# One-hot rows of the expert gates: from three engines to two, with their keys in PSUM

## The chip, the cores and the metric

The kernel runs on one core of a Trainium2 chip. Five engines work beside each other, each through its own queue in order: TensorE (PE, matrix products), VectorE (DVE), ScalarE (ACT), GpSimd (POOL) and SyncE (SP, which only issues transfers). The metric is the device time of one execution in microseconds, median of several runs.

## The reference, cut to what matters

One decoder block on 1024 tokens of width 1024 (with 16 meta tokens ahead): a convolution branch and an RWKV-7 branch, mixed by gates, and then a product-key expert layer (PEER). Only the last concerns the change. Each token has 8 heads; each head picks 16 of 16384 experts by two keys of 128, so a token has 128 pairs of an expert `e = i1 * 128 + i2` and a gate.

```python
e = (i1 * PEER_NKEYS + i2).reshape(TOK_BLOCK, PEER_HEADS * K)
gate = jax.nn.softmax(best_s, axis=-1).reshape(TOK_BLOCK, PEER_HEADS * K)
u = expert_u[e]
act = jax.nn.gelu(jnp.einsum('td,ted->te', xb, u), approximate=False)
coef = (gate * act.astype(jnp.float32)).astype(xb.dtype)
return jnp.einsum('te,ted->td', coef, expert_v[e])
```

## The kernel before, in words

The 1024 tokens are 8 tiles of 128, in two halves: tiles 0 to 3 and 4 to 7. The front part of the block and the routing (`mix_and_route`, with `top16` and `route`) run for the first half, then for the second. The expert layer is then done in two ways.

Tiles 0 to 2 are gathered (`gather_rows`): for each of a token's 128 experts an indirect transfer issued by GpSimd (L1002) brings the expert's two rows; VectorE multiplies one with the token and sums (L1005, the row product), ScalarE makes the gelu and the gate (L1006, L1007), VectorE adds the other row times the result (L997, the row sum). Tile 0's gather has the lowest priority, so it fills what the routing and the spread leave; it must be done before the dense part, which puts tile 3's result in tile 0's buffer (`hr3` under the tag `hr0`).

Tiles 4 to 7 and tile 3 are done densely: products with all 16384 experts in 128 blocks of 128, and gates that are zero but for 128 of them. For tiles 4 to 7 `u_stage` computes gelu(x u) of a block; 56 of the 128 blocks (`PRE`) are computed ahead and stored (`gs`). Tile 3's activations are computed by gathering (`gather_coefs`) and lie, times its gates, in `coef`.

`spread_gates` (L1042 on) makes the dense gates, and is what the change edits. For each tile it transposes the expert's two keys and the gates (`src[0]`, `src[1]`, `src[2]`), and for each token multiplies two one-hot matrices on TensorE: `o2` has a one where the second key is, `o1` the gate where the first key is. Work goes in quartets of four tokens, 32 quartets a tile, 160 in all. One VectorE instruction (L1076) compares `src[1]` of four tokens with `iota`, the numbers 0 to 127 in SBUF. The four `o1` rows are compared and scaled one by one (L1085): of tiles 4 to 7 (`hf` is 1) VectorE makes two, GpSimd the third, and ScalarE the fourth in two steps, an absolute difference (L1082) and a Relu (L1083); of tile 3 VectorE makes three and GpSimd one. Four products (L1087) go to one PSUM bank, `pg`, which ScalarE evicts (L1088) to `gt`, the 32 tokens of a group side by side. A group's first blocks are copied to `direct` tiles (L1090), the rest is written to DRAM (`gd`, L1091). The tiles come in the order 4, 5, 6, 7, 3 (`DT`).

The dense part (`dense`) takes four blocks at a time, multiplies the activations with the gates (L1134), splits the product into two parts for TensorE (`split`: ScalarE L224, then GpSimd L225) and adds the products with the experts' rows (L1161). Its tiles take over the memory in which the spread's lay.

Products at full precision take three passes (`mm3`, L228 to L230) over operands that ScalarE and GpSimd have split; `ul` and `vlo` are such low parts, made by GpSimd.

The order of each engine's queue is fixed when the program is built: a planner simulates the program, takes for each engine the ready instruction that stands first in program order (shifted by `high_priority` offsets), and adds waits where tiles depend on each other. So `PRE` blocks, the spread and tile 0's gather are interleaved by the planner's own times.

Of the kernel before, what the change touches and what calls it, by code (L numbers as in the profile page):

```python
# [10 lines left out]
F32 = mybir.dt.float32  # L11
# [3 lines left out]
AF = mybir.ActivationFunctionType  # L15
OP = mybir.AluOpType
# [4 lines left out]
P = 128  # L21
# [15 lines left out]
DT = list(range(4, 8)) + list(range(NGT, 4))  # L37
# [95 lines left out]
def body(tc, a, out):  # L133
    nc = tc.nc
    V, A, G, PE, SY = nc.vector, nc.scalar, nc.gpsimd, nc.tensor, nc.sync

    def pool(es, name, bufs=1, space=None, side=None):
        kw = {}
        if space is not None:
            kw["space"] = space  # L140
        if side is not None:
            kw["side"] = side
        return es.enter_context(tc.tile_pool(name=name, bufs=bufs, reuse_waits="tile", **kw))
# [40 lines left out]
    iota = cst[:, C_IOTA:C_IOTA + P]  # L184
# [858 lines left out]
    def spread_gates(es, direct):  # L1043

        gtp = pool(es, "gtp", 2)
        sb = pool(es, "sg_", 2)
        ps_ = pool(es, "sgp", 2, PSUM)
        for s_, tt in enumerate(DT):
            hf, tl = divmod(tt, 4)
            src = []  # L1050
            for k in range(3):
                f = sb.tile([P, P], F32, name="gsrc", tag="gsrc")
                if k < 2:
                    ii = sb.tile([P, P], I32, name="gint", tag="gint")
                    V.tensor_single_scalar(ii, idx[hf][:, tl], 7 if k == 0 else 127,
                                           op=OP.logical_shift_right if k == 0 else OP.bitwise_and)
                    V.tensor_copy(f, ii)
                else:
                    f = gate[1][:, tl] if hf else coef[0]
                pt = ps_.tile([P, P], F32, name="gtp")  # L1060
                PE.transpose(pt, f, ident)
                ft = sb.tile([P, P], F32, name=f"gT{k}")
                A.activation(ft, pt, AF.Copy)  # L1063
                src.append(ft)
            neg = []
            for k in (0, 2):
                nt = sb.tile([P, P], F32, name=f"ng{k}")
                V.tensor_scalar_mul(nt, src[k], -1.0)
                neg.append(nt)
            for g in range(P // GT):  # L1070
                gt = gtp.tile([P, P, GT], F32, name="gt")
                for q in range(GT // 4):
                    pg = ps_.tile([P, 4, P], F32, name="pg", bufs=3)
                    t0 = GT * g + 4 * q
                    o2 = sb.tile([P, 4, P], F32, name="o2h", bufs=3)
                    V.tensor_tensor(o2, src[1][:, t0:t0 + 4, None].to_broadcast([P, 4, P]),  # L1076
                                    iota[:, None, :].to_broadcast([P, 4, P]), op=OP.is_equal)
                    o1 = sb.tile([P, 4, P], F32, name="o1h", bufs=3)
                    for x in range(4):
                        t = t0 + x  # L1080
                        if x == 3 and hf:
                            A.activation(o1[:, x], iota, AF.Abs, bias=neg[0][:, t:t + 1])  # L1082
                            A.activation(o1[:, x], o1[:, x], AF.Relu, scale=neg[1][:, t:t + 1], bias=src[2][:, t:t + 1])  # L1083
                        else:
                            (G if x >= 2 + (not hf) else V).tensor_scalar(o1[:, x], iota, src[0][:, t:t + 1], src[2][:, t:t + 1],  # L1085
                                                               op0=OP.is_equal, op1=OP.mult)
                        PE.matmul(pg[:, x], o2[:, x], o1[:, x], start=True, stop=True)  # L1087
                    A.activation(gt[:, :, 4 * q:4 * q + 4].rearrange("p i t -> p t i"), pg, AF.Copy)  # L1088
                for k, d in enumerate(direct):
                    A.activation(d[:, P // GT * s_ + g], gt[:, GB * k:GB * k + GB], AF.Copy)  # L1090
                A.dma_start(gd[P // GT * s_ + g][:, GB * len(direct):], gt[:, GB * len(direct):])  # L1091
# [137 lines left out]
    with ExitStack() as e0:  # L1229
        spread_gates(e0, direct)  # L1230
# [21 lines left out]
```

## Time and profile before

| | us |
|---|---|
| median of three runs | 3814.73 (3814.04 to 3827.25) |
| the profiled execution, its own time | 3849.75 |
| its span, first to last instruction | 3848.0 |

The profile is of one execution. A group's row gives line, engine, operation, tiles (written <- read), shape, count, then busy time in us with the mean ns of one, then the engine's idle time before them with what ended it. A row of a line's own view gives shortest, median and longest in ns. A row of the timeline gives start and length in us, and in brackets idle time before it. A row of stretches gives length and the busy time and count of TensorE's products, its weight loads, VectorE, ScalarE and GpSimd, then the granted TensorE clock, the share of the transfer engines and GB/s.

### The profile page before, as it was taken

Reading aid. Unit: us, or ns where it says so; the run is one execution under the profiler, and the core shown is the slowest. Engines: PE = TensorE matmul, PEld = TensorE weight load, DVE = VectorE, ACT = ScalarE, POOL = GpSimd, SP = SyncE. Lnnn points to the kernel's source line nnn. Section 1 sums busy time; section 2 is a strip of 40 time slices with the busy share of each in tenths; the row PEclk is TensorE's granted clock in tenths of the full one; section 3 lists DMA queues with packets and bytes.
Section 4 is the critical chain, followed back from the end, with each engine's and each line's share of the span. In section 5 each row is a group of like instructions: output and inputs, shape, how many; then the busy total and the mean of one; then the engine's idle time right before and its main releaser. Section 6 shows DMA issues by size and latency. Waiting matters only on the chain. (4 is left out here: it accounts for less than half of the span.)

```text
span 3848.0 us, 49366 instructions
## 1 busy us (share of the span) xinstructions
PE 3378.2 (88%) x16175; PEld 2692.2 (70%) x16175; DVE 2784.9 (72%) x5150; ACT 1602.1 (42%) x3647; POOL 2405.1 (63%) x2123
## 2 busy tenths in 40 slices
PE   7999998798889987788788885899989999889997
PEld 7887775686667765676677764777777777667776
DVE  3655549789986668899999997666666666656763
ACT  5455432334443332432377764333333343333343
POOL 3442315446786548556799996666766666666773
PEclk9999978999897878989899997999999999999998
DMA  4321114424676668744677777888888878888993
GB/s 150 108 62 52 53 50 141 138 79 157 211 228 213 189 232 307 268 151 170 224 284 270 286 274 276 302 292 306 317 301 311 310 279 299 298 307 309 333 311 107
DMA packets 343126, 861.38 MB, mean 224 GB/s; under 512 B 53304, under 2 KB 132800, under 8 KB 290900
## 3 DMA queue, kind: packets, MB, share of 16 engines
q0 software_dynamic: 75328, 475.06, 34.6%
q1 hardware_dynamic: 252420, 322.48, 26.4%
q10 hardware_dynamic: 15120, 60.68, 4.0%
q8 instruction: 128, 2.10, 0.2%
q14 instruction: 130, 1.06, 0.1%
HBM read 774.33 MB, written 83.77 MB: 223 GB/s over the span
## 5 line engine op out<-in xcount | busy, mean ns | idle before, releaser
L1002 POOL DMA_INDIRECT row<-euv,idx x384 | 422.4, 1100 | 345.7 <-DVE yr L997 168.9
L225 POOL TENSOR_TENSOR vlo<-vraw,vhi 128x512 fp32r<-128x512 f32 x256 | 327.9, 1295 | 235.7 <-ACT vhi L224 215.6
L1005 DVE SCALAR_TENSOR_TENSOR row<-row,xr 128x1024 f32<-128x1024 f32 x256 | 311.5, 1218 | 179.0 <-DMA row<-euv,idx 168.9
L997 DVE SCALAR_TENSOR_TENSOR yr<-row,act,yr 128x1024 f32<-128x1024 f32 x256 | 329.6, 1288 | 153.1 <-ACT act L1007 146.4
L1006 ACT ACTIVATE act<-act 128x1 f32<-128x1 f32 x384 | 77.0, 200 | 813.8 <-DVE row L1005 813.4
L225 POOL TENSOR_TENSOR ul<-ur,uh 128x512 fp32r<-128x512 f32 x256 | 337.4, 1325 | 41.3 <-ACT uh L224 39.4
L228 PE MATMUL py<-vhi,c 128*128 128x512 f32 x640 | 265.7, 420 | 87.0 <-DVE hbuf L1161 45.2
L230 PE MATMUL zp<-x,ul 128*128 128x512 f32 x736 | 299.4, 407 | 20.6 <-POOL ul L225 20.6
L228 PE MATMUL zp<-x,uh 128*128 128x512 f32 x736 | 298.9, 406 | 4.9 <-ACT g L1099 4.8
L229 PE MATMUL zp<-x,uh 128*128 128x512 f32 x736 | 297.7, 404 | 0.0
L228 PE MATMUL zp<-vhi,c 128*128 128x512 f32 x640 | 254.0, 406 | 29.6 <-DVE hbuf L1161 22.5
L230 PE MATMUL py<-vhi,c 128*128 128x512 f32 x640 | 259.9, 412 | 21.8 <-POOL c L225 21.8
L224 ACT ACTIVATE vhi<-vraw 128x512 fp32r<-128x512 f32 x256 | 159.0, 626 | 270.7 <-DMA vraw<-euv 126.6
L229 PE MATMUL py<-vlo,c 128*128 128x512 f32 x640 | 262.9, 411 | 4.5 <-POOL vlo L225 4.5
L1087 PE MATMUL pg<-o1h,o2h 128*128 128x128 f32 x1280 | 198.8, 295 | 70.3 <-DVE o1h L1085 39.9
L229 PE MATMUL zp<-vlo,c 128*128 128x512 f32 x640 | 254.3, 401 | 0.1
L1085 POOL TENSOR_SCALAR o1h<-cst,gT,gT 128x128 f32<-128x128 f32 x160 | 249.5, 1563 | 7.1 <-ACT gT L1063 3.1
L230 PE MATMUL zp<-vhi,c 128*128 128x512 f32 x640 | 251.9, 402 | 0.0
L1087 PEld LDWEIGHTS pg<-o1h,o2h 128*128 128x128 f32 x1280 | 179.0, 202 | 100.3 <-POOL o1h L1085 37.7
L349 DVE SCALAR_TENSOR_TENSOR cy<-u,vec,cy 128x512 f32<-128x512 f32 x240 | 242.2, 1009 | 5.4
L997 DVE SCALAR_TENSOR_TENSOR hr<-row,act,hr 128x1024 f32<-128x1024 f32 x128 | 212.5, 1660 | 30.1 <-ACT act L1007 29.6
L1024 POOL DMA_INDIRECT row<-euv,twice x128 | 157.5, 1231 | 118.5 <-DVE row L1026 77.0
(1646 smaller groups left out, 9732.4 us busy)
## 6 DMA issues: line engine op xcount, KB each, us to landing
ur<-eut SPq DMA_DIRECT2D x256, 256.0 KB, 5.9
vraw<-euv SPq DMA_DIRECT2D x256, 256.0 KB, 5.7
gd<-gt ACTq DMA_DIRECT2D x20, 1920.0 KB, 7.9
gblk<-gd SPq DMA_DIRECT2D x30, 1024.0 KB, 16.2
wbr<-w_in SPq DMA_DIRECT2D x64, 256.0 KB, 3.3
wqr<-w_q SPq DMA_DIRECT2D x64, 256.0 KB, 2.9
wrr<-w_in SPq DMA_DIRECT2D x56, 256.0 KB, 2.7
gs<-g SPq DMA_DIRECT2D x56, 256.0 KB, 4.3
```

The costliest lines, as they stand in the source:

```text
L224: A.activation(hi, src, AF.Copy)
L225: return eng.tensor_sub(lo, src, hi.bitcast(F32))
L228: PE.matmul(ps, whi, xhi, start=first, stop=False)
L229: PE.matmul(ps, whi, xlo, start=False, stop=False)
L230: PE.matmul(ps, wlo, xhi, start=False, stop=last)
L349: V.scalar_tensor_tensor(y, u[:, j:j + 512], cw, y, op0=OP.mult, op1=OP.add)
L997: V.scalar_tensor_tensor(y, row[:, 1], act[:, j:j + 1], y, op0=OP.mult, op1=OP.add)
L1002: G.indirect_dma_start(out=row.rearrange("p a d -> p (a d)"), out_offset=None, in_=a["euv"], in_offset=bass.IndirectOffsetOnAxis(ap=idx[0] ...
L1005: V.scalar_tensor_tensor(row[:, 0], row[:, 0], 1.0, xn, op0=OP.mult, op1=OP.mult, accum_out=aj)
L1024: G.indirect_dma_start(out=row, out_offset=None, in_=a["euv"].rearrange("e (k d) -> (e k) d", k=2), in_offset=bass.IndirectOffsetOnAxis(ap ...
L1085: (G if x >= 2 + (not hf) else V).tensor_scalar(o1[:, x], iota, src[0][:, t:t + 1], src[2][:, t:t + 1], op0=OP.is_equal, op1=OP.mult)
L1087: PE.matmul(pg[:, x], o2[:, x], o1[:, x], start=True, stop=True)
```

## The change

A PSUM tile `keys` gets a copy of `iota`; all comparisons of the spread read it. GpSimd's rows are made by VectorE: three of four in tiles 4 to 7, all four in tile 3. The tiles come in the order 3, 4, 5, 6, 7 (each keeps its slot `s_` in the gates). The eviction's two patterns are exchanged: it reads `pg` with a stride and writes runs of four neighbouring words, where it read in order and wrote single words 32 apart.

```diff
         ps_ = pool(es, "sgp", 2, PSUM)
-        for s_, tt in enumerate(DT):
+        keys = ps_.tile([P, P], F32, name="keys", bufs=1)
+        A.activation(keys, iota, AF.Copy)
+        for s_, tt in sorted(enumerate(DT), key=lambda x: x[1]):
...
                     V.tensor_tensor(o2, src[1][:, t0:t0 + 4, None].to_broadcast([P, 4, P]),
-                                    iota[:, None, :].to_broadcast([P, 4, P]), op=OP.is_equal)
+                                    keys[:, None, :].to_broadcast([P, 4, P]), op=OP.is_equal)
...
                         if x == 3 and hf:
-                            A.activation(o1[:, x], iota, AF.Abs, bias=neg[0][:, t:t + 1])
+                            A.activation(o1[:, x], keys, AF.Abs, bias=neg[0][:, t:t + 1])
                             A.activation(o1[:, x], o1[:, x], AF.Relu, scale=neg[1][:, t:t + 1], bias=src[2][:, t:t + 1])
                         else:
-                            (G if x >= 2 + (not hf) else V).tensor_scalar(o1[:, x], iota, src[0][:, t:t + 1], src[2][:, t:t + 1],
-                                                               op0=OP.is_equal, op1=OP.mult)
+                            V.tensor_scalar(o1[:, x], keys, src[0][:, t:t + 1], src[2][:, t:t + 1], op0=OP.is_equal, op1=OP.mult)
                         PE.matmul(pg[:, x], o2[:, x], o1[:, x], start=True, stop=True)
-                    A.activation(gt[:, :, 4 * q:4 * q + 4].rearrange("p i t -> p t i"), pg, AF.Copy)
+                    A.activation(gt[:, :, 4 * q:4 * q + 4], pg.rearrange("p t i -> p i t"), AF.Copy)
```

## Rows read from the trace of the kernel before

**Rows 1.** The page's part 1: busy us, share of the span, instructions.
```profile
span 3848.0 us, 49366 instructions
...
PE 3378.2 (88%) x16175; PEld 2692.2 (70%) x16175; DVE 2784.9 (72%) x5150; ACT 1602.1 (42%) x3647; POOL 2405.1 (63%) x2123
```
**Rows 2.** Busy time by stretch: second routing, spread, seam, dense part.
```profile
1650.00:1901.00 251.00, 204.84 (x816) 161.41 (x815) 249.46 (x859) 77.46 (x159) 154.88 (x99) 0.89 0.51 173
1901.00:2342.00 441.00, 369.23 (x2088) 313.61 (x2087) 427.44 (x698) 317.28 (x675) 412.07 (x281) 0.95 0.75 273
2342.00:2390.00 48.00, 22.14 (x76) 16.79 (x77) 30.41 (x33) 16.79 (x41) 25.52 (x23) 0.67 0.91 331
2390.00:3790.00 1400.00, 1284.29 (x5341) 1026.74 (x5340) 901.19 (x1197) 487.68 (x1232) 945.82 (x885) 0.96 0.86 301
```
**Rows 3.** Groups by shape in the spread's stretch, 1901 to 2342 us.
```profile
L1085 POOL TENSOR_SCALAR o1h<-cst,gT,gT 128x128 f32<-128x128 f32 x160 | 249.5, 1563 | 7.1 <-ACT gT L1063 3.1 <-issue 1.2 <-PE pg L1087 1.2
...
L1088 ACT ACTIVATE gt<-pg 128x512 f32<-128x512 f32 x160 | 173.4, 1090 | 40.6 <-PE pg L1087 40.2
L1085 DVE TENSOR_SCALAR o1h<-cst,gT,gT 128x128 f32<-128x128 f32 x352 | 163.0, 514 | 0.0
L1076 DVE TENSOR_TENSOR o2h<-gT,cst 128x512 f32<-128x512 f32 x160 | 147.5, 923 | 4.4 <-PE pg L1087 4.4
...
L1082 ACT ACTIVATE o1h<-cst,ng 128x128 f32<-128x128 f32 x128 | 47.1, 369 | 1.0 <-DVE ng L1068 1.0
```
**Rows 4.** Line L1087: what TensorE sat idle for before it (us, times).
```profile
  POOL o1h L1085: 65.5, 80
  DVE o1h L1085: 48.3, 50
```
**Rows 5.** Lines' own views, 1901 to 2342 us: shortest, median, longest ns.
```profile
L1085 DVE TENSOR_SCALAR o1h<-cst,gT,gT x352: 331/364/2211, 1910.6 to 2338.2; 128x128 f32<-128x128 f32 x176
...
L1076 DVE TENSOR_TENSOR o2h<-gT,cst x160: 673/680/3793, 1901.7 to 2337.0; 128x512 f32<-128x512 f32 x160
...
L997 DVE SCALAR_TENSOR_TENSOR hr<-row,act,hr x53: 1269/1274/3078, 1899.9 to 2338.4; 128x1024 f32<-128x1024 f32 x53
...
L1005 DVE SCALAR_TENSOR_TENSOR row<-row,xng x54: 1207/1212/4334, 1906.0 to 2341.9; 128x1024 f32<-128x1024 f32 x54
```
**Rows 6.** Timeline, 1993 to 1997 us: two on VectorE, one on GpSimd.
```profile
1993.36 0.59 DVE L1085 TENSOR_SCALAR o1h<-cst,gT,gT 128x128 f32<-128x128 f32 x2
...
1994.48 2.47 DVE L1085 TENSOR_SCALAR o1h<-cst,gT,gT 128x128 f32<-128x128 f32 x2
...
1995.49 1.30 POOL L225 TENSOR_TENSOR ul<-ur,uh 128x512 fp32r<-128x512 f32 x1
```
**Rows 7.** VectorE groups of the whole span, then two lines' own views.
```profile
L1134 DVE TENSOR_TENSOR g<-g,gblk 128x512 f32<-128x512 f32 x56 | 49.1, 877 | 83.8 <-DMA g<-gs 83.5
...
L1134 DVE TENSOR_TENSOR g<-py,gblk 128x512 f32<-128x512 f32 x36 | 24.8, 688 | 12.2 <-ACT py L1099 9.1 <-POOL c L225 2.5 <-issue 0.4
...
L474 DVE TENSOR_SCALAR m<-pp x12: 159/676/692, 79.3 to 1205.5; 128x512 f32<-128x512 f32 x8, 128x16 f32<-128x16 f32 x4
...
L347 DVE TENSOR_SCALAR cy<-u,vec x8: 531/932/1655, 151.1 to 680.7; 128x512 f32<-128x512 f32 x8
```
**Rows 8.** Groups by shape in the second routing, 1650 to 1901 us.
```profile
L997 DVE SCALAR_TENSOR_TENSOR hr<-row,act,hr 128x1024 f32<-128x1024 f32 x21 | 44.6, 2124 | 1.3 <-ACT act L1007 1.3
...
L1005 DVE SCALAR_TENSOR_TENSOR row<-row,xng 128x1024 f32<-128x1024 f32 x20 | 31.5, 1573 | 0.0
```
**Rows 9.** Timeline at 2350 us: VectorE's last part of a product, then ScalarE.
```profile
2350.33 0.08 DVE L1005 DVE_READ_ACCUMULATOR row<-row,xng 128x1 f32 x1
...
2350.45 0.20 ACT L1006 ACTIVATE act<-act 128x1 f32<-128x1 f32 x1 [6.78 <-DVE row L1005]
```
**Rows 10.** A ScalarE eviction with contiguous ends, group of the whole span.
```profile
L961 ACT ACTIVATE qT<-acc 128x512 f32<-128x512 f32 x32 | 18.6, 581 | 0.0
```
**Rows 11.** The chain of waits, 2330 to 2400 us: start, length, what.
```profile
2341.61 11.30 DMA gd<-gt
```

## The prediction

> **What bounds the kernel now.** The page first: of a span of 3848 us VectorE is busy 72% and TensorE 88%, so no engine bounds the whole [rows 1]. A table of busy time by stretch says where the change falls. The spread of the gates lies between 1901 and 2342 us; there VectorE is busy 427 of 441 us, GpSimd 412, TensorE 369, ScalarE 317. VectorE was already full before it, in the second half's routing (249.5 of 251 us from 1650), and has room again only when the dense part runs (901 of 1400), where TensorE is the full engine (1284 of 1400) [rows 2]. So from 1650 to 2342 time is VectorE's sum of instructions, whatever their order, and a microsecond off that sum moves the start of the dense part, and with it the end, by one.
>
> Next, that stretch's groups by shape: what is VectorE's sum made of? 352 one-hot rows `o1h` and 160 one-hot tiles `o2h`, besides 54 row products and 53 row sums of tile 0's gather; GpSimd makes 160 `o1h` at 1563 ns each [rows 3, 5]. The waits of the spread's matmuls name both makers: 65.5 us until a GpSimd `o1h`, 48.3 us until a VectorE one [rows 4]. Those 65.5 us are no gain by themselves: TensorE has 72 us of slack in the stretch.
>
> What makes VectorE's sum larger than its work: the mean of each group stands far above its median. `o1h` 514 against 364 ns, `o2h` 923 against 680 [rows 3, 5]. In order of time the cause is seen: two `o1h` take 0.59 us at 1993.36, the next two 2.47 us, and they end when the `ul` split on GpSimd, begun at 1995.49, ends [rows 6]. The excess in this stretch is (514 - 364) x 352 = 52.8 us and (923 - 680) x 160 = 38.9 us: 92 us of 441.
>
> **The change, part by part.**
>
> *Keys in PSUM: the stalls go.* That a VectorE instruction with one input in PSUM escapes them is shown by the gates' multiply: with both inputs in SBUF it takes 877 ns, with one in PSUM 688, in the same stage beside the same GpSimd work [rows 7]. Bounds of the gain: 0 (the stalls follow the output, not the input) to 92 us; I take all 92, as the row is of the same kind.
>
> *Keys in PSUM: each read is slower.* 512 elements in SBUF with two per-partition scalars take 531 ns at best, 128 take 331 [rows 5, 7]: 0.52 ns an element. From PSUM 512 elements take 676 ns, 16 take 159 [rows 7]: 1.04 ns. So an `o1h` gains 128 x 0.52 = 67 ns, from 336 to 403. `o2h` is a two-input operation at 1.04 ns an element already: no change. 352 x 0.067 = 23.6 us. Bounds: 0 and 46 us (twice).
>
> [...]
>
> *160 rows come over from GpSimd.* In a run VectorE starts the second of two `o1h` 0.26 us after the first (0.59 less 0.33) [rows 6]; with 0.067 it is 0.32 us. 160 x 0.32 = 51.2 us. Together: -92 + 24 + 51 = **-17 us**. GpSimd loses 249.5 us of work [rows 3]; what it keeps, gather issues and splits, was nowhere the bound, so this is worth nothing in itself.
>
> *Fourth tile first.* Its gates don't come from the second half's routing, so its spread may start while routing still fills VectorE. It frees nothing there, but takes the place of gather rows, whose priority is lowest. Those cost most there: a row sum 2124 ns and a product 1573, against medians of 1274 and 1212 later [rows 5, 8]: 21 x 0.85 + 20 x 0.36 = 25 us. Bounds 0 (buffers held by the routing keep the tile waiting) and 25; I take half, **-12 us**. Nothing of the dense part gets later by it: after the last eviction `gd`'s write still stands in the way for 11.3 us, because the dense part's tiles lie where `gt` lay [rows 11]. TensorE is idle there; the first two products of gates and `g`, which now wait for the last tile, take 0.69 us each [rows 7] and fit in.
>
> *ScalarE's `Abs` reads the same bank.* If its reads of `keys` are put in order with VectorE's, the change adds a wait: `Abs` of a quartet after VectorE's third `o1h`, and VectorE's next `o2h` after that `Abs`. Queued behind the waiting `o2h` is all of VectorE, rows included unless the planner put one in between. A handover costs 0.04 us each way (a product ends at 2350.41, ScalarE starts 2350.45) [rows 9]. With a gather row in the gap I charge only two handovers: 128 x 0.08 = **+10 us**. Rows suffice: 53 sums and 54 products [rows 5] for 128 gaps.
>
> *Evictions.* 160 at 1.09 us write words 32 apart; the nearest with contiguous ends takes 0.58 [rows 3, 10]. Now PSUM is read with a stride instead: no row shows it. Bounds 0.58 and 1.60 us (both penalties); I take 0.65, nearer the contiguous row. ScalarE, at 317 of 441 us, hides either; without cover the upper end is 82 us on ScalarE.
>
> Sum: -17 - 12 + 10 = **-19 us**, all on VectorE's path. Against the profiled execution's own 3849.8 us that is 3830; the median of the runs is 35 us below it, so 3814.7 - 19 = 3796 us.
>
> **Rivals.**
>
> *The two readers alternate (slower).* In each of 128 quartets VectorE waits for `Abs`: 0.37 us [rows 3], two handovers, and the overlap of 0.08 us that a dependent instruction loses: 0.53 us; ScalarE, 72% busy, adds some 0.2. Unfilled that is 128 x 0.73 = 93 us against 29 saved: +64. It decides from about 40 unfilled gaps (40 x 0.73 = 29). For it: ScalarE's queue is in order too, so a late `Abs` also holds evictions back; the planner knows neither the stalls nor, perhaps, the eviction's real time, so its rows may fall beside the gaps. Against: as many rows as gaps. With two thirds unfilled, +33: 3848 us. [...]
>
> *No difference.* What is won is lost again: the tile starts no earlier, -17 + 10 = -7; or a read from PSUM costs twice the 67 ns, 512 x 0.067 = 34 us more on the forecast, +15. That is 3808 to 3830 us. The PSUM row speaks against the second [rows 7]. [...]
>
> *Larger gain.* All 25 us of dear rows leave the routing, the readers are not ordered, and the last gather rows slip under the write of `gd`: -17 - 25 - 13 = -55, 3760 us. TensorE's slack (72 us) allows it. Against: it takes all three.
>
> **How the numbers follow.** Forecast (3775 to 3812): 0.45; alternating readers: 0.30; no difference: 0.12; larger gain: 0.13. What a measurement can tell from no change is 0.5%, 19 us, so the forecast itself lies on that line. Faster: 0.25 of the forecast, 0.13, and 0.02 of the third, 0.40. Same: 0.20, 0.04 of the alternation (gaps half filled), 0.08: 0.32. Slower: 0.26 and 0.02: 0.28. Range for 8 in 10: 3755 (all gains) to 3860 (three quarters of the gaps open); the forecast's own range is 3775 to 3812.
>
> **What would show it.** `o1h` on VectorE x512 at a mean near 400 ns and hardly above its median, `o2h` at 680; no GpSimd instruction at the one-hot line; row products and sums with a mean still above the median. The first `o2h` before 1895 us if the tile's head start works. Waits of VectorE's `o2h` for ScalarE's `Abs`, by their count and total, decide between forecast and alternation: under 30 us for the forecast. Evictions near 0.65 us. The last matmul of the spread near 2320 instead of 2340 us. Wrong, if the spread's stretch is longer than 441 us, if `o1h` from PSUM has a median over 470 ns, or if VectorE is idle in it for more than 50 us.

## The result, and the profile after

The changed kernel takes 3851.9 us (median of 11 runs, 3827.6 to 3871.3); the kernel before, timed beside it, 3821.3 (11 runs, 3806.2 to 3835.3). The ratio is 1.0074, 95% interval 1.0046 to 1.0103: **slower by 28 us** (the medians differ by 31), where 19 us less were forecast. The time is near that of the first rival, in which the two readers alternate (3848 us).

The page of the profile after, part 1, to compare with [rows 1]:
```profile
span 3858.2 us, 49060 instructions
...
PE 3409.8 (88%) x16175; PEld 2717.4 (70%) x16175; DVE 2759.2 (72%) x5310; ACT 1567.0 (41%) x3648; POOL 2150.0 (56%) x1963
```
GpSimd lost 255 us and ScalarE 35 us of work, VectorE 26 us. Nobody works more except TensorE, whose 16175 products took 32 us more at a lower granted clock (0.914 over the span, 0.922 before; see the last section), and yet the execution is longer. So the loss is first looked for as idle time in the stage that was changed.

The profiled spans differ by 10 us only, because the profile of before fell above all of its timed runs, and what lies ahead of the stored blocks differs by up to 39 us between the traces (their first product starts at 1681 to 1720 us). So kernels are compared here over a stretch that every trace has: from the first product of the stored blocks (`zp` from the second half) to the last product of the spread, and from there to the first product of the dense part (`py`). Busy time of the two stretches before (columns as in [rows 2]):
```profile
1720.00:2340.50 620.50, 516.19 (x2664) 427.98 (x2662) 606.44 (x1223) 371.24 (x786) 530.26 (x355) 0.94 0.69 247
2340.50:2362.10 21.60, 0.02 (x2) 0.02 (x1) 13.02 (x15) 6.05 (x20) 9.65 (x9) 0.50 0.95 361
```
The same two after, and as third row the end of the first:
```profile
1717.00:2369.90 652.90, 555.29 (x2664) 456.23 (x2662) 605.84 (x1400) 341.96 (x806) 287.68 (x203) 0.88 0.68 250
2369.90:2382.10 12.20, 0.04 (x1) 0.00 (x0) 8.58 (x11) 8.30 (x20) 4.27 (x5) 0.54 0.60 224
2283.00:2370.00 87.00, 69.91 (x320) 55.75 (x320) 64.60 (x158) 58.88 (x130) 0.64 (x2) 0.83 0.35 143
```
The first stretch grew by 32.4 us. VectorE's busy time in it is the same (606.4 and 605.8), its idle time rose from 14.1 to 47.1 us: the stretch is longer because VectorE waits. The same sum of work hides an exchange: the one-hots take 25 us less, and 74 row sums and 73 products lie in the stretch, 19 us more than the 68 of each before; the rest of the work in it is 5 us more. The seam (from the spread's last product to the dense part's first) gave 9.4 us back: five products and five sums of tile 0 lay in it before, and now tile 0 is done long ahead of it. The third row shows where most of the waiting is: for the last 87 us GpSimd has next to nothing to do (0.6 us), the transfers are at 143 GB/s, and VectorE is idle for 22 us.

What VectorE waited for, its groups after, 1650 to 2420 us:
```profile
L1087 DVE TENSOR_SCALAR o1h<-keys,gT,gT 128x128 f32<-128x128 f32 x512 | 176.7, 399 | 0.0
L1005 DVE SCALAR_TENSOR_TENSOR row<-row,xng 128x1024 f32<-128x1024 f32 x78 | 122.0, 1564 | 13.4 <-DMA row<-euv,idx 13.2
L997 DVE SCALAR_TENSOR_TENSOR hr<-row,act,hr 128x1024 f32<-128x1024 f32 x79 | 119.6, 1514 | 1.6 <-ACT act L1007 1.6
L1078 DVE TENSOR_TENSOR o2h<-gT,keys 128x512 f32<-128x512 f32 x160 | 108.8, 680 | 28.4 <-ACT o1h L1084 28.0 <-issue 0.4
```
L1084 is ScalarE's `Abs`: 28.0 us. The one-hot instructions have no stall left: `o1h` 399 ns (514 in [rows 3]) and `o2h` 680 (923).

The line of `o2h` by itself in the last 87 us, its durations and what ended VectorE's idle time before it (us, times):
```profile
L1078 DVE TENSOR_TENSOR o2h<-gT,keys x39: 686/687/689, 2283.8 to 2366.8; 128x512 f32<-128x512 f32 x39
...
  ACT o1h L1084: 20.9, 39
```
All 39 quartets wait, 0.54 us each. Of the 121 before them, 32 (tile 3's) have no `Abs`, and the other 89 wait 16 times. The difference is the gather rows: on VectorE nothing else is left to fill a gap. The line of the row products shows when they ran out:
```profile
L1005 DVE SCALAR_TENSOR_TENSOR row<-row,xng x78: 1196/1218/3462, 1650.6 to 2270.5; 128x1024 f32<-128x1024 f32 x78
```
Tile 0's last product starts at 2270.5 us, 99 us before the spread ends. Before, one still ended at 2350.41 [rows 9], after the spread. In order of time the tail looks like this (timeline at 2320 us; in brackets idle time and what ended it):
```profile
2319.63 0.72 DVE L1087 TENSOR_SCALAR o1h<-keys,gT,gT 128x128 f32<-128x128 f32 x2
...
2320.39 0.37 ACT L1084 ACTIVATE o1h<-keys,ng 128x128 f32<-128x128 f32 x1
2320.78 0.69 DVE L1078 TENSOR_TENSOR o2h<-gT,keys 128x512 f32<-128x512 f32 x1 [0.43 <-ACT o1h L1084]
...
2321.39 1.04 DVE L1087 TENSOR_SCALAR o1h<-keys,gT,gT 128x128 f32<-128x128 f32 x3
2322.16 0.60 ACT L1089 ACTIVATE gt<-pg 128x512 f32<-128x512 f32 x1 [0.89 <-PE pg L1088]
2322.66 0.36 ACT L1084 ACTIVATE o1h<-keys,ng 128x128 f32<-128x128 f32 x1
2323.05 0.69 DVE L1078 TENSOR_TENSOR o2h<-gT,keys 128x512 f32<-128x512 f32 x1 [0.62 <-ACT o1h L1084]
```
VectorE's third `o1h` ends at 2322.43. `Abs` could follow, but an eviction stands ahead of it in ScalarE's queue, so that it starts at 2322.66. It ends at 2323.02, and `o2h`, which waited 0.62 us for it, starts at 2323.05.

ScalarE's groups after, 1880 to 2380 us, give the other direction and the evictions:
```profile
L1089 ACT ACTIVATE gt<-pg 128x512 f32<-128x512 f32 x160 | 94.0, 591 | 58.3 <-PE pg L1088 56.0 <-DVE idx L841 1.7
...
L1084 ACT ACTIVATE o1h<-keys,ng 128x128 f32<-128x128 f32 x128 | 46.9, 367 | 59.6 <-DVE o1h L1087 58.8
```
`Abs` waits 58.8 us for VectorE's `o1h`, for which it waited not at all before [rows 3]; an eviction takes 591 ns instead of 1090 [rows 3].

### The profile page after: what moved, and what is told of

Same layout as the page of the kernel before. It is cut to its first block, busy times and chain, and to the rows that moved or that the text cites. A ratio compares the mean times of both kernels' runs of the same rounds, so it can differ in the third digit from the quotient of the medians.

```text
span 3858.2 us, 49060 instructions
## 1 busy us (share of the span) xinstructions
PE 3409.8 (88%) x16175; PEld 2717.4 (70%) x16175; DVE 2759.2 (72%) x5310; ACT 1567.0 (41%) x3648; POOL 2150.0 (56%) x1963
## 3 DMA queue, kind: packets, MB, share of 16 engines
q14 instruction: 127, 1.04, 0.1%
## 4 chain that ended last, share of the span: by engine, by line
PE 25%; DVE 20%; DMA 15%; issue 13%; POOL 8%; ACT 2%; SPq 1%; POOLq 0%; DVEq 0%; ACTq 0%
DMA row<-euv,idx 7%; DMA vraw<-euv 4%; PE zp L228 4%; PE zp L229 3%; PE zp L230 3%; DVE row L1005 2%; PE py L228 2%; DMA g<-gs 2%; DVE hr L997 2%; PE py L229 2%; PE py L230 2%; POOL vlo L225 2%; PE pg L1088 1%; POOL row L1002 1%; POOL row L1024 1%
## 5 line engine op out<-in xcount | busy, mean ns | idle before, releaser
L1002 POOL DMA_INDIRECT row<-euv,idx x384 | 412.2, 1073 | 530.4 <-DVE yr L997 238.8
L1088 PE MATMUL pg<-o1h,o2h 128*128 128x128 f32 x1280 | 251.1, 334 | 73.9 <-DVE o1h L1087 46.4
L230 PE MATMUL zp<-x,ul 128*128 128x512 f32 x736 | 297.7, 404 | 11.4 <-POOL ul L225 11.3
L1088 PEld LDWEIGHTS pg<-o1h,o2h 128*128 128x128 f32 x1280 | 219.3, 227 | 119.7 <-issue 40.6
L1005 DVE SCALAR_TENSOR_TENSOR row<-row,xng 128x1024 f32<-128x1024 f32 x128 | 204.0, 1594 | 34.0 <-DMA row<-euv,idx 33.8
L1026 DVE SCALAR_TENSOR_TENSOR row<-row,xng 128x1024 f32<-128x1024 f32 x128 | 185.2, 1454 | 57.1 <-DMA row<-euv,twice 56.7
```

Of the source, the lines that this page charges most:

```text
L230: PE.matmul(ps, wlo, xhi, start=False, stop=last)
L1002: G.indirect_dma_start(out=row.rearrange("p a d -> p (a d)"), out_offset=None, in_=a["euv"], in_offset=bass.IndirectOffsetOnAxis(ap=idx[0] ...
L1005: V.scalar_tensor_tensor(row[:, 0], row[:, 0], 1.0, xn, op0=OP.mult, op1=OP.mult, accum_out=aj)
L1026: V.scalar_tensor_tensor(row, row, 1.0, xn, op0=OP.mult, op1=OP.mult, accum_out=act[:, j:j + 1])
```

## The experiments

Each was timed beside the kernel before, whose median was 3821.6, 3822.2 and 3824.7 us in the three groups of runs; ratios are to that kernel, and differences in us are between medians where nothing else is said. "Theory 1" is that the order of the two readers is the loss; its rivals are the order in which the filling work runs out, and VectorE's sum.

**1. `Abs` from SBUF, all else as changed.**
```diff
-                            A.activation(o1[:, x], keys, AF.Abs, bias=neg[0][:, t:t + 1])
+                            A.activation(o1[:, x], iota, AF.Abs, bias=neg[0][:, t:t + 1])
```


> The changed kernel, but ScalarE's Abs reads the numbers in SBUF, so VectorE is the only reader of the PSUM keys. Theory 1 (the two readers alternate, and this is the loss): the 28.0 us in which VectorE's o2h waited for Abs and the 58.8 us in which Abs waited for VectorE's o1h vanish; the spread ends some 28 us earlier, near 2342 us, and the time is near 3824 us, level with the kernel before. Theory 2 (the loss is the order of the fillers: the stored blocks and tile 0's gather run out early and leave the last 97 us of the spread alone): the waits vanish too, but the tail is still alone and is bound by another latency; at most 10 us come back, 3842 us or more. Theory 3 (VectorE's sum of instructions grew by the rows from GpSimd): no change, 3852 us.

3807.0 us, ratio 0.9965 (0.9944 to 0.9985): 45 us off the changed kernel (42 by the ratios), more than the 28 us of visible waits and than the 28 us expected. The stretch to the last product of the spread is
```profile
1714.30:2319.80 605.50, 521.60 (x2664) 441.32 (x2662) 598.75 (x1398) 322.08 (x800) 279.21 (x200) 0.91 0.74 263
```
and VectorE's groups of the row products and of `o2h`, 1650 to 2420 us, are
```profile
L1005 DVE SCALAR_TENSOR_TENSOR row<-row,xng 128x1024 f32<-128x1024 f32 x77 | 120.6, 1567 | 4.7 <-DMA row<-euv,idx 4.7
...
L1078 DVE TENSOR_TENSOR o2h<-gT,keys 128x512 f32<-128x512 f32 x160 | 108.2, 676 | 0.0
```
VectorE is idle for 6.8 us instead of 47.1. Of these 40 us, 28 were waits for `Abs` and some 9 waits of row products for their transfers (13.4 against 4.7). The two profiled executions themselves lie 36 us apart. The second theory (the fillers' order by itself) and the third (VectorE's sum) fall: with the readers apart the gather lasts to the end of the spread again (its last product starts at 2315.5 us), so its running out was a consequence of the filled gaps.

**2. The readers in two banks.** The transposes at a tile's start give up one of their two banks.
```diff
+        keya = ps_.tile([P, P], F32, name="keya", bufs=1)
+        A.activation(keya, iota, AF.Copy)
...
-                pt = ps_.tile([P, P], F32, name="gtp")
+                pt = ps_.tile([P, P], F32, name="gtp", bufs=1)
...
-                            A.activation(o1[:, x], keys, AF.Abs, bias=neg[0][:, t:t + 1])
+                            A.activation(o1[:, x], keya, AF.Abs, bias=neg[0][:, t:t + 1])
```


> The changed kernel, but ScalarE's Abs reads a second copy of the keys in a PSUM bank of its own; the bank comes from the transposes at a tile's start, which get one instead of two. Theory (what costs is that two engines' reads of one bank are put in order): no waits between o2h and Abs, 3807 us as with Abs from SBUF, within 8 us. Rival (an Abs from PSUM is itself what delays VectorE or ScalarE): 3852 us.

3808.2 us, 0.9961 (0.9939 to 0.9984): the same as from SBUF. So ScalarE's read of PSUM costs nothing here (`Abs` takes 362 ns on average, 393 from SBUF in experiment 1, and `o2h` does not wait for it); the shared tile in one bank does (28.0 us of waits). The copy and its bank came together here, so which of the two sharings makes the order is not shown.

**3. The old order of the tiles**, in the changed kernel and, second, with `Abs` from SBUF.
```diff
-        for s_, tt in sorted(enumerate(DT), key=lambda x: x[1]):
+        for s_, tt in enumerate(DT):
```


> The changed kernel with the tiles in the old order 4, 5, 6, 7, 3. As predicted, the head start is worth 12 us, so its loss costs that: 3864 us. Rival: the head start only exchanges gather rows against quartets and is worth nothing; and since tile 3 has no ScalarE row, it comes last as a tail without alternation, where 39 waits of 0.54 us (20.9 us) stood: 3852 - 21 = 3831 us.

> The changed kernel with Abs from SBUF and the tiles in the old order, so that the order is seen without the two readers. Theory (the head start is worth nothing, as it was beside the alternation): the time of the order-new twin, 3807 us, within 8 us. Rival as predicted: the head start is worth 12 us, 3819 us. Third: the old order is the better one without the alternation, since tile 3 has the longest sum on VectorE and the spread of the others then hides it: 3795 us.

3848.9 us, 1.0079 (1.0048 to 1.0109), and 3807.6 us, 0.9964 (0.9936 to 0.9993): each as its twin in the new order (3851.9 and 3807.0). The head start is worth nothing that can be told: the intervals of the two pairs together leave an estimated 10 us either way. A tail without alternation (tile 3 last) doesn't help either: in the first of the two VectorE's waits for `Abs`, in the four other tiles, are still 19.1 us, and those of row products for their transfers 17.7; the last row product starts at 2229.8 us, and the spread's last product at 2344.

**4. The new evictions alone**, in the kernel before.
```diff
-                    A.activation(gt[:, :, 4 * q:4 * q + 4].rearrange("p i t -> p t i"), pg, AF.Copy)
+                    A.activation(gt[:, :, 4 * q:4 * q + 4], pg.rearrange("p t i -> p i t"), AF.Copy)
```


> The kernel before with the new eviction patterns alone. Evictions take 0.60 us instead of 1.09, ScalarE loses 160 x 0.49 = 78 us of work. Theory as predicted: ScalarE is not the bound in the spread, so no change, within 5 us of the kernel before. Rival: the 40.2 us in which evictions waited for products and the held pg buffers passed on to TensorE and VectorE, so that up to 20 us are gained.

3821.2 us, 0.9992 (0.9966 to 1.0019): no change.

**5. PSUM keys for VectorE alone**, GpSimd's rows and `Abs` from SBUF, old order; first with the old evictions, then with those of 4. The `keys` tile and `o2h` are as in the change.
```diff
-                            (G if x >= 2 + (not hf) else V).tensor_scalar(o1[:, x], iota, src[0][:, t:t + 1], src[2][:, t:t + 1],
-                                                               op0=OP.is_equal, op1=OP.mult)
+                            g_ = x >= 2 + (not hf)
+                            (G if g_ else V).tensor_scalar(o1[:, x], iota if g_ else keys, src[0][:, t:t + 1], src[2][:, t:t + 1],
+                                                           op0=OP.is_equal, op1=OP.mult)
```


> The kernel before with the keys in PSUM for VectorE alone: GpSimd keeps its 160 rows and ScalarE its Abs, both from SBUF; old order, old evictions. VectorE's o1h near 400 ns and o2h near 680, stalls gone: 92 - 24 = 68 us off VectorE's sum. Theory as predicted: VectorE is the bound, so the spread ends some 68 us earlier as far as GpSimd's own rows allow (412 us of work in 441): between -30 and -68 us, 3753 to 3791. Rival: GpSimd's rows (65.5 us of TensorE's idle time) and the tail behind them are the bound as soon as VectorE is not: gain under 15 us, 3806 us or more.

> Of the change only the PSUM keys for VectorE and the new evictions; GpSimd keeps its rows and ScalarE its Abs, both from SBUF, in the old order. Theory (evictions are off the path, as they were in the kernel before): 3780 us, within 8, as with the keys alone. Rival (with VectorE shorter, ScalarE's 395 us are near the bound and the 78 us that the evictions free now count): 3765 us or less.

3780.3 us, 0.9904 (0.9875 to 0.9934), and 3779.0 us, 0.9890 (0.9854 to 0.9926). This part of the change by itself **gains 37 to 46 us** (41 and 46 by the medians, 37 and 42 by the ratios). GpSimd's one-hot rows in their line's own view (shortest, median, longest ns) took before
```profile
L1085 POOL TENSOR_SCALAR o1h<-cst,gT,gT x160: 787/1367/3279, 1908.1 to 2332.9; 128x128 f32<-128x128 f32 x160
```
and here, in the second of the two,
```profile
L1088 POOL TENSOR_SCALAR o1h<-cst,gT,gT x160: 782/807/3052, 1867.2 to 2246.5; 128x128 f32<-128x128 f32 x160
```
The stalls were mutual: GpSimd's own rows, which nobody changed, fall from a median of 1367 to 807 ns, and from a mean of 1563 to 1203 (from 1880 to 2300 us), so some stalls are left.

**6. GpSimd's rows to VectorE alone**, in the kernel before, all keys in SBUF.
```diff
-                            (G if x >= 2 + (not hf) else V).tensor_scalar(o1[:, x], iota, src[0][:, t:t + 1], src[2][:, t:t + 1],
-                                                               op0=OP.is_equal, op1=OP.mult)
+                            V.tensor_scalar(o1[:, x], iota, src[0][:, t:t + 1], src[2][:, t:t + 1], op0=OP.is_equal, op1=OP.mult)
```


> The kernel before with GpSimd's 160 rows made by VectorE, keys still in SBUF for all. Prices from the runs so far: 160 more rows at some 0.26 us in a run are 42 us, and the stalls that GpSimd's work puts on VectorE's SBUF operations go down by what GpSimd's rows caused of them. If GpSimd's 250 us of rows caused the stalls in proportion to their share of its 412 us: 92 x 0.6 = 55 us back, so 3821 + 42 - 55 = 3808 us, faster or the same. If the splits with two inputs (ul) cause them, as the prediction said: all stalls stay and hit 160 more rows, 3821 + 42 + 24 = 3887 us, clearly slower.

3821.9 us, 0.9996 (0.9972 to 1.0021): between the two expectations. GpSimd's rows make stalls: without them the mean of `o2h` is 768 ns instead of 923 [rows 3]. What GpSimd keeps, splits and gather issues, may make others (the stall of [rows 6] ends with a split), but no run separates it: 768 is still above the median of 680. Beside its twin with PSUM keys (the second of 3, which also has the new evictions, worth nothing by 4) it shows what the keys do when VectorE makes all these rows. VectorE's groups, 1650 to 2420 us, keys in SBUF:
```profile
L1085 DVE TENSOR_SCALAR o1h<-cst,gT,gT 128x128 f32<-128x128 f32 x512 | 213.5, 473 | 0.0
L1076 DVE TENSOR_TENSOR o2h<-gT,cst 128x512 f32<-128x512 f32 x160 | 122.8, 768 | 0.0
L997 DVE SCALAR_TENSOR_TENSOR hr<-row,act,hr 128x1024 f32<-128x1024 f32 x79 | 120.5, 1526 | 2.2 <-ACT act L1007 2.2
L1005 DVE SCALAR_TENSOR_TENSOR row<-row,xng 128x1024 f32<-128x1024 f32 x77 | 100.6, 1306 | 0.7 <-DMA row<-euv,idx 0.7
```
and keys in PSUM:
```profile
L1087 DVE TENSOR_SCALAR o1h<-keys,gT,gT 128x128 f32<-128x128 f32 x512 | 176.4, 399 | 0.0
L997 DVE SCALAR_TENSOR_TENSOR hr<-row,act,hr 128x1024 f32<-128x1024 f32 x77 | 124.8, 1621 | 1.9 <-ACT act L1007 1.9
L1005 DVE SCALAR_TENSOR_TENSOR row<-row,xng 128x1024 f32<-128x1024 f32 x76 | 116.5, 1533 | 4.9 <-DMA row<-euv,idx 4.8
L1078 DVE TENSOR_TENSOR o2h<-gT,keys 128x512 f32<-128x512 f32 x160 | 108.1, 675 | 0.0
```
The one-hots lose 52 us (336.3 to 284.5), and the gather rows, which still read two inputs from SBUF, take 20 us of that back (221.1 to 241.3, for three rows fewer). The time falls by 14 us.

**7. The two readers with GpSimd's rows back at GpSimd.** As the second of 5, but `Abs` reads the keys in PSUM.
```diff
-                            A.activation(o1[:, x], iota, AF.Abs, bias=neg[0][:, t:t + 1])
+                            A.activation(o1[:, x], keys, AF.Abs, bias=neg[0][:, t:t + 1])
```

> The changed kernel with GpSimd's 160 rows back at GpSimd (from SBUF) and the old order; Abs still reads the keys in PSUM. It asks whether the order of the two readers costs its 45 us wherever it stands. Theory (each open gap is a handover and an Abs, 0.54 us, on VectorE's path; rows run out before the spread ends): 3780 + 45 = 3825 us, within 12. Rival (VectorE has 128 rows less between two Abs and GpSimd's rows are late anyway, so the order hides behind GpSimd): under 3800 us.

3805.0 us, 0.9957 (0.9929 to 0.9985), 26 us above its twin. VectorE's waits for `Abs` were 19.0 us here. The order of the readers costs in this setting too, though less than the 45 us expected; which part of the difference GpSimd's rows hide is open.

**8. Towards a better version.** The second of 3, and ScalarE makes two rows of each quartet (one in tile 3). It leaves out the negative gates, which only tile 3 has: for these the Relu gives zero at the key and, by its formula, positive numbers two or more keys away, so those rows do not hold the reference's numbers.
```diff
-                        if x == 3 and hf:
+                        if x >= 3 - hf:
```


> Towards a better version: keys in PSUM for VectorE alone, Abs from SBUF, new evictions, old order; GpSimd's rows go to ScalarE instead of VectorE: two of four in tiles 4 to 7, one of four in tile 3 (288 instead of 128 pairs of Abs and Relu at 0.86 us: 138 us more, against 78 us that the new evictions free). VectorE makes 352 rows as before the change. Theory (VectorE's sum is the bound, ScalarE has room: 310 + 60 = 370 us of some 400): at the level of the keys-for-VectorE-alone kernel or better, 3770 to 3785 us. Rival (ScalarE's queue becomes the bound, since a pair and an eviction stand in one order): 3800 us or more.

3773.5 us, 0.9865 (0.9823 to 0.9906). With tile 3's fourth row on GpSimd instead (all gates kept):
```diff
-                        if x == 3 and hf:
+                        if x >= 2 and hf:
...
-                            V.tensor_scalar(o1[:, x], keys, src[0][:, t:t + 1], src[2][:, t:t + 1], op0=OP.is_equal, op1=OP.mult)
+                            g_ = x == 3
+                            (G if g_ else V).tensor_scalar(o1[:, x], iota if g_ else keys, src[0][:, t:t + 1], src[2][:, t:t + 1],
+                                                           op0=OP.is_equal, op1=OP.mult)
```


> A better version: PSUM keys for VectorE alone, new evictions, old order; in tiles 4 to 7 ScalarE makes two rows of four from SBUF and VectorE two, GpSimd none; in tile 3 VectorE makes three and GpSimd the fourth. VectorE's sum is that of the kernel with 352 rows and GpSimd is almost free. Theory: as the kernel with 288 ScalarE rows, 3773 us, within 8. Rival (tile 3's GpSimd rows at the end, at 1.25 us each, hold TensorE up): 3785 us or more.

3765.7 us, 0.9848 (0.9816 to 0.9880): 59 us faster than the kernel before and 86 below the changed one. Against the second of 5 (0.9890) the intervals overlap. Last, one more row goes from VectorE to GpSimd in tiles 4 to 7:
```diff
-                            g_ = x == 3
+                            g_ = x == (1 if hf else 3)
```

> As the version with two ScalarE rows, but in tiles 4 to 7 GpSimd makes the second row too, so that VectorE makes one of four (224 rows in all instead of 352; 128 less at 0.32 us are 41 us off its sum; GpSimd takes 160 rows at 1.25 us). Theory (VectorE's sum is still the bound): 20 to 40 us below the version before, 3735 to 3755. Rival (ScalarE, at 350 of some 390 us, or TensorE is the bound by now): within 8 us of 3773 or above.

3803.3 us, 0.9943 (0.9922 to 0.9965): worse. VectorE is no longer the bound. The stretch to the last product of the spread is
```profile
1700.30:2306.40 606.10, 516.29 (x2664) 433.42 (x2662) 542.37 (x1114) 396.37 (x1062) 475.82 (x362) 0.93 0.74 266
```
and before the spread's products TensorE sat idle (us, times) until
```profile
  POOL o1h L1088: 26.2, 36
  ACT o1h L1085: 22.8, 18
  ACT gt L1091: 21.5, 21
  ACT o1h L1084: 21.0, 13
  DVE o1h L1088: 19.4, 21
```
VectorE is idle for 64 us; the waits are spread over all makers, and what ties them together was not tried.

## Why the prediction was wrong

**The step that failed** is "With a gather row in the gap I charge only two handovers", and with it "Rows suffice: 53 sums and 54 products for 128 gaps": +10 us were charged, 45 measured (experiment 1, and 44 by 2). Three things were wrong in it. By its own count there were 107 rows for 128 gaps. Rows were counted over the whole stretch, but each row that fills an early gap is gone for a late one; they were used up at 2274 us, and the last 39 gaps stood open at 0.54 us. And rows drawn ahead come sooner than their transfers: 13.4 us of waits for them. The wait in an open gap was about right: in the rival `Abs` and two handovers are 0.45 us, and 0.65 with ScalarE's other work. That the rival's 3848 us came near the time is luck in its terms: it set 62 us of waits against 29 saved, and 45 and 14 were measured.

**Keys in PSUM and GpSimd's rows** were to give -17 us together; experiments 1, 2 and the second of 3 give -13 to -15 by their ratios. That is close by two errors that cancel: the keys were to give -68 (-92 and +24) and gave -37 to -46 by themselves (experiment 5), the rows were to cost 51 and cost 29. The terms inside: `o1h` 403 ns forecast, 399 measured; `o2h` 680 and 680. The rows from GpSimd cost VectorE 51.3 us of `o1h` time (125.1 us in the second of 5, 176.4 in the second of 3) against 51.2 forecast; in time the two differ by 29 us. "I take all 92" held for the one-hots, `o1h` and `o2h`: they fell from 310.5 [rows 3] to 285.5 us, 25 less where 17 were forecast (stalls were counted above a median of 364 ns, the new cost from 336, so 352 x 0.028 = 10 us fell between). It left out the gather rows. Before, from 1650 to 2420 us, these were
```profile
L997 DVE SCALAR_TENSOR_TENSOR hr<-row,act,hr 128x1024 f32<-128x1024 f32 x79 | 130.4, 1651 | 5.4 <-ACT act L1007 5.0
L1005 DVE SCALAR_TENSOR_TENSOR row<-row,xng 128x1024 f32<-128x1024 f32 x78 | 112.8, 1446 | 11.4 <-DMA row<-euv,idx 11.4
```
243.2 us, and 241.6 after: GpSimd's rows gone take 22 us off them (221.1 in experiment 6), the keys in PSUM put 20 back. Experiments 5 and 6 show where the stalls stay: the row products, with two SBUF inputs, stay dear with the one-hots' keys in PSUM (1533 ns on average, where the shortest took 1207 [rows 5]), and GpSimd's median falls from 1367 to 807 ns once VectorE's one-hots read PSUM. What makes the two engines hold each other up is not shown.

**Fourth tile first**: -12 forecast, 0 measured (experiment 3, twice). The tile did start early (first `o2h` at 1820.3 us, 1901.7 in [rows 5]), but "takes the place of gather rows" failed. VectorE's groups after in the routing, 1650 to 1901 us, against [rows 8]:
```profile
L1005 DVE SCALAR_TENSOR_TENSOR row<-row,xng 128x1024 f32<-128x1024 f32 x19 | 38.9, 2049 | 0.0
L997 DVE SCALAR_TENSOR_TENSOR hr<-row,act,hr 128x1024 f32<-128x1024 f32 x19 | 31.3, 1645 | 1.6 <-ACT act L1007 1.6
...
L1087 DVE TENSOR_SCALAR o1h<-keys,gT,gT 128x128 f32<-128x128 f32 x24 | 8.3, 396 | 0.0
...
L1078 DVE TENSOR_TENSOR o2h<-gT,keys 128x512 f32<-128x512 f32 x6 | 4.0, 665 | 0.0
```
Only six quartets came ahead, as many as the three buffers each of `pg` and `o2h` hold: the first eviction starts at 1901.3 us only, released by the routing's `idx` (the 1.7 us in its group above). That fits the prediction's own lower bound, "buffers held by the routing keep the tile waiting". The six displaced three rows of 41. The rest of those rows are as dear as before (70.2 us against 76.1).

**Evictions**: 0.65 us taken, 0.59 measured, and no gain (experiment 4), as argued.

**The sum from the runs**, by medians: -14 (keys and rows), 0 (order), +45 (readers), 0 (evictions), in all +31; measured +31 (28 by the ratio). It closes by construction, as the 45 is the changed kernel less experiment 1. Measured apart, the readers cost 44 (experiment 2), 41 in the old order (3) and 26 with GpSimd's rows at GpSimd (7).

**The bound.** "Time is VectorE's sum of instructions, whatever their order" held for the sum but not for the end: rows that lie in the seam are in part hidden behind the write of `gd` (11.3 us [rows 11]), rows drawn ahead are not. Experiment 1 shows it without the alternation. Against the kernel before its stretch is 15.0 us shorter: the one-hots take 25 us less, but 18 us more of rows lie in it, and 7 are idle time saved. Its seam is 22.5 us with no row of tile 0 left in it (the chain of waits there is the next tile's transfers `xng`, 11.4 us, and `y`, 7.2), and 21.6 before with ten. So of 25 us off VectorE's sum 7 or 8 shortened the stretch. Of the tests, the spread's stretch (1901 to 2370, 469 us against 441) rightly spoke against the forecast. The test "under 30 us for the forecast" was badly chosen: the waits are 28.0 us, on the forecast's side, though the alternation is what happened; and the idle time, 47.1 us, stayed just under the 50 that were to speak against it. A wait that was filled with work from later isn't seen where it was filled, only where that work is missing.

## What to carry to other kernels

A tile that VectorE and ScalarE both read cost an order between them here, even between reads (28.0 us of waits, 45 us in time); give each engine its own copy (here in a bank of its own), or let only the one that gains read it. Filling work covers a wait only as long as it lasts: ask when it runs out, not how much of it there is. And a change of several parts should be taken apart before it is judged: here one part was worth about 41 us, and two others, 29 and 45 us, lost more than that.

## What the runs showed of the hardware

A VectorE comparison of 128 elements takes 399 ns (median after the change) with its keys in PSUM and 335 (median, experiment 6) from SBUF, so a PSUM source costs some 64 ns here. That it is the elements is an estimate: it rests on the prediction's 0.52 and 1.04 ns each, by which 128 elements cost 67 ns more, and on `o2h`, which gains nothing from a PSUM source (a median of 679 ns after, 680 from SBUF in experiment 6). No run compares at another length.

ScalarE reads PSUM with a stride of 128 words at next to no cost: 591 ns on average for 512 elements, against 581 with contiguous ends [rows 10]. What cost 1090 ns before was the write of single words 32 apart.

TensorE's granted clock was lower once the stored blocks had run out (their last product starts at 2172 us, before the change at 2287): 0.98 or more from 1901 to 2100 us, 0.56 from 2200 to 2300, where products took 65.6 us of 100 (0.94 and 84.5 us there before the change), and 0.83 in the tail. Why it fell is not shown. Its products of the spread took 334 ns on average, 295 before. With the waits for `Abs` gone (experiment 1) the blocks end as early (2176 us) and the clock falls too, to 0.71 from 2200 to 2300 us, but VectorE is busy for 98.1 of these 100: this lower clock alone does not hold it up. What the step from 0.71 to 0.56 adds to the waits is open.
